# A hybrid encoder layer on one core: which half of a unit runs first, and when the fourth sums of the merged tiles are split

## The chip, the cores and the metric

The kernel runs on one core of a Trainium2 chip. What counts is device time in microseconds (us), from one launch to its end; lower is better. The engines in this text: PE (TensorE, matmuls), DVE (VectorE), ACT (ScalarE), POOL (GpSimd) and SP (SyncE, which issues most DMAs).

## What is computed

One layer over 512 tokens of width 2048, in float32:

```python
hn = rmsnorm(x, norm_g)
proj = jnp.einsum('bsd,dc->bsc', hn, w_in)       # 2048 -> 12 x 512 columns, 4 logits, 3 x 2048 gates
ya = forgetting_attention(qa, ka, va, f_logit)   # three branches of 4 heads of 128
yb = chunked_relpos_attention(qb, kb, vb, rel_bias)
yc = stick_breaking_attention(qc, kc, vc)
ys = jnp.stack([from_heads(ya), from_heads(yb), from_heads(yc)], axis=2)
ys = ys * jax.nn.silu(br[:, :, :, 3])
up = jnp.einsum('bsnw,nwd->bsnd', ys, w_up)      # per branch 512 -> 2048
merged = jnp.sum(gates * up, axis=2)
return x + jnp.einsum('bsd,de->bse', merged, w_out)
```

Nearly all of the work is in three projections: w_in, w_up and w_out.

## The kernel before

**Precision.** A float32 operand is used as a high and a low part (hi and lo; weights: tiles wh and wl). ACT makes the high part by a copy that rounds, DVE subtracts it from the source and so makes the low one (`split`, L243 to L251). A product is hi x hi + hi x lo + lo x hi.

**Units.** PE's work on weights is a list of units. A unit is one 128-column block of weights over eight blocks of 128 rows. For each of the eight, one wide matmul takes wh against the 256 high and 256 low columns of the moving operand (512 columns, into both halves of a PSUM bank), and one narrow matmul takes wl against the 256 high ones (256 columns, into the left half). All eight wide ones run first, then the eight narrow ones. DVE later folds the two halves of the bank together.

**Tasks of seven.** w_in and w_out are multiplied by a Strassen-like scheme (`PairTask`): for two column blocks, two halves of the rows and two halves of the tokens it makes seven products, 1 to 7, instead of eight, so a task is seven units. Products 1, 2, 5, 6, 7, 3, 4 take sums of weights (made by POOL's accumulating DMAs and by DVE in `sums`) against sums of the moving operand. Its usual order is 1, 2, 6, 5, 7, 3, 4. Products 6, 7, 4 and 3 are summed onto the bank that product 1, 6, 7 and 5 left open (`onto`); 1, 2 and 5 open a bank of their own. Two tasks, the first gate task and the first output task, are "late": each product has a bank of its own, and its wh runs as 16 narrow matmuls; the last task ends with one such product (`single`).

**Moving operands.** For w_in these are x1, x2, t23 and t4; for w_out they are m1, m2, m23 and m4 of the merged gates x up (a tile for each of eight pairs of blocks k). The first three of a pair are `Parts` tiles with both token halves; the fourth sum has one half, so two k shared one `Parts` tile. There are 28 tiles for `Parts`; they come free as the tiles of ys are done with (`up_half` for six of them, `up_done` for six more).

**Stages.** First head (in quarters), then heads and gates over w_in (to about 1036 us), then w_up: 16 blocks d in the order k, k + 8 of 36 wide matmuls each, with the gates read back from DRAM (sg) and multiplied in; then eight output tasks from about 1164 us to the end. `merged_a(k)` runs behind block k and `merged_b(k)` behind block k + 8. `merged_b` makes m2, the two third sums (in mt) and the fourth (in mu), waits for `up_half` or `up_done`, splits the third sums into m23 and, after `up_done`, the fourth ones into m4 (`late_t4`).

**The order.** A planner inside the kernel (`Flow`) writes the program: every piece of work is a generator that names its engine, a cost and what it waits for, and the planner keeps a clock for each engine and picks what starts first, by due time. A smaller slack means an earlier due time. PE, DVE and ACT then run exactly in the order written; only semaphores decide when. `stream` walks the units and spawns the preparation (`prep`: wh, then wl) two units ahead.

Of the kernel before, what the change touches and what calls it, by code (L numbers as in the profile page):

```python
# [9 lines left out]
F32R = mybir.dt.float32r  # L10
# [6 lines left out]
S = 512  # L17
# [8 lines left out]
UK = 8  # L26
NQ = 4
HS = S // 2
# [7 lines left out]
PE, ACT, DVE = 0, 1, 2  # L36
# [26 lines left out]
class Flow:  # L63
# [85 lines left out]
def mm_us(n, x=1):  # L149
    return x * max(0.115, n / 2400 + 0.0133)  # L150
# [11 lines left out]
def hybrid_kernel(  # L162
# [31 lines left out]
    flow = Flow()  # L194
    spawn, set_, give = flow.spawn, flow.set, flow.give
# [3 lines left out]
    def t2(s, dt=F32):  # L199
        return tp.tile([P, S], dt, tag="t2", name=nm(s))  # L200
# [19 lines left out]
    def two(ap):  # L220

        return ap.rearrange("p (h s) -> p h s", h=2)
# [19 lines left out]
    def split(hi, lo, src, n, ev=None, due=(), hi_ev=None):  # L242

        yield (ACT, act_us(n), *due)
        nc.scalar.activation(hi, src, AF.Copy)  # L245
        if hi_ev is not None:
            set_(hi_ev)
        yield (DVE, dve_us(n), *due)
        nc.vector.tensor_sub(lo, src, f(hi))  # L249
# [13 lines left out]
    def mm(ps, w, x, start=False, stop=False, more=False):  # L263
        nc.tensor.matmul(ps, w, x, start=start, stop=stop, skip_group_check=more)  # L264
# [87 lines left out]
    class Unit:  # L352


        def __init__(self, mms, after=None, shape=(UK, P), srcs=()):
            self.shape, self.mms, self.after, self.srcs = list(shape), mms, after, srcs
            self.ready_hi, self.ready, self.there, self.raw = Event(), Event(), Event(), None

        def source_there(self):
            return self.there  # L360
# [208 lines left out]
    class Pair(Unit):  # L569


        def __init__(self, task, i):
            super().__init__(task.mms_of(i), task.after_of(i))
            self.task, self.p = task, task.order[i]

        def source_there(self):
            if self is self.task.units[0]:
                spawn(self.task.sums(), 3.0)
            return self.task.there[self.p]

        def source(self):
# [6 lines left out]
    class PairTask:  # L588
# [57 lines left out]
        def mms_of(self, i):  # L646
            p = self.order[i]
            bank = (0, 1, 2, 0, 0, 1, 2)[i] if self.late else {2: 1, 5: 2, 3: 2}.get(p, 0)
            onto = None if self.late else {6: 1, 7: 6, 4: 7, 3: 5}.get(p)
            more = onto is not None  # L650
            single = self.late or self.plain_end and p == 4
            self.bank = getattr(self, "bank", {})
            self.bank[p] = bank

            def go(u):
                if more:
                    yield self.ev[onto]
                    self.ps[p] = self.ps[onto]
                else:
                    yield accs[bank], 1  # L660
                    self.ps[p] = acc(bank)

                for j in range(UK):
                    yield lambda: self.ops[p](j) is not None
                    r, _, ev = self.ops[p](j)
                    yield ev
                    if single:
                        yield PE, mm_us(HS)
                        mm(self.ps[p][:, LH], u.hi[:, j, :], r[:, 0, :], j == 0 and not more, more=more)
                    else:  # L670
                        yield PE, mm_us(S)
                        mm(two(self.ps[p]), u.hi[:, j, :], r, j == 0 and not more, more=more)
                    if single:
                        yield PE, mm_us(HS)
                        mm(self.ps[p][:, LH], u.hi[:, j, :], r[:, 1, :], more=more)
                yield u.ready
                for j in range(UK):
                    yield PE, mm_us(HS)
                    mm(self.ps[p][:, LH], u.lo[:, j, :], self.ops[p](j)[1], stop=j == UK - 1, more=more)
            return go  # L680

        def after_of(self, i):
# [701 lines left out]

        return [Unit(mms(i), shape=(6, P), srcs=[w_up[d, i]]) for i in range(2)]

    m1, m2, m23, m4 = [None] * UK, [None] * UK, [None] * UK, [None] * (UK // 2)
    m4_ev = [Event() for _ in range(UK // 2)]
    kept_m, m1_ev, mus, up_half, up_done = {}, [Event() for _ in range(UK)], {}, Event(), Event()

    def merged_a(k, a):

# [39 lines left out]
    def late_t4(k, u, due):  # L1432
        if k % 2 == 0:
            yield xps, 1
            m4[k // 2] = Parts("m4")
            set_(m4_ev[k // 2])
        yield m4_ev[k // 2]
        h, lo, ev = m4[k // 2].half(k % 2)
        yield from split(h, lo, u, HS, ev, (due + 14.0,))
        if k % 2:  # L1440
            give(t2s)

    for k in range(UK):
        for d in (k, k + UK):
# [4 lines left out]
    at(len(units), freed(xps, 6, up_done))  # L1449


    mops = strassen_ops(m1, m2, m23, m4)

    def out_pair(e):
        evs = [Event(), Event()]
# [71 lines left out]
            yield from load_unit(u)  # L1527

    def stream():
        for i, u in enumerate(units):  # L1530
            cur[0] = i
            for g in side.pop(i, ()):
                spawn(g(), 5.0, flow.fin)
            for j in range(LA + 1) if i == 0 else (i + LA,):
                if j < len(units):
                    spawn(prep(units[j]), 2.5, flow.fin)
            yield u.ready_hi
            yield from u.mms(u)
            if u.after is not None:
                spawn(u.after(), 0.0, flow.fin)  # L1540
# [79 lines left out]
```

## Time and profile before

| | |
|---|---|
| median of 3 runs | 1327.93 us (1326.29 to 1328.51) |
| the profiled execution | 1328.65 us, of it 1326.9 from the first to the last instruction (the span) |
| matmuls | 7506 |
| busy: weight loads, DVE, ACT, POOL | 87%, 86%, 61%, 7% of the span |
| granted TensorE clock | 1.0 all along |
| DMA | 266.24 MB, 201 GB/s on average |

A busy time is the sum of an engine's instruction times. PE's matmuls overlap in its pipeline, so that the busy share says little by itself; the start times of consecutive matmuls say how long one holds up the next. In the views, a row of the timeline is a start in us, a busy time in us, the engine, the line, the tiles (out<-in), and how many instructions the row merges; in brackets stands how long the engine was idle before, and what ended the idle time.

### The profile page before, as it was taken

To read this page: it belongs to the slowest core of one execution; us is meant where nothing else is said; L and a number is where in the kernel's file an instruction comes from. 1 tells how busy PE (TensorE), PEld (TensorE's weight loads), DVE (VectorE), ACT (ScalarE), POOL (GpSimd) and SP (SyncE) were. 2 spreads that over 40 slices of the span, in tenths; PEclk is the share of its full clock that TensorE was granted. 3 is DMA by queue.
4 is the path that set the end of the run, shared out by engine and by line. 5 is a ranking of instruction groups with operands and counts; after the bars stand their busy time and mean duration, and the time that the engine had idled before them with its cause. 6 is when DMAs were issued, how large, how long until landed. Compare 5 with 4: busy or idle time off the path is not lost.

```text
span 1326.9 us, 20238 instructions
## 1 busy us (share of the span) xinstructions
PE 1320.2 (99%) x7506; PEld 1150.5 (87%) x7506; DVE 1134.7 (86%) x1676; ACT 805.9 (61%) x1280; POOL 94.9 (7%) x120
## 2 busy tenths in 40 slices
PE   9999999999999999999999999999999999999998
PEld 6898888888888888888888888888888888888887
DVE  8989888788888889888898979888898877897786
ACT  8767657575556665666656665666557655454443
POOL 0000001000010100000000000000000000001000
PEclk9999999999999999999999999999999999999999
DMA  9776776767786776867878777776779755668893
GB/s 336 207 206 168 190 198 176 212 177 190 200 203 172 197 201 181 219 160 207 200 182 215 173 193 201 192 196 181 194 178 272 278 194 184 193 172 243 235 254 94
DMA packets 89651, 266.24 MB, mean 201 GB/s; under 512 B 10560, under 2 KB 12608, under 8 KB 89552
## 3 DMA queue, kind: packets, MB, share of 16 engines
q1 hardware_dynamic: 70400, 203.86, 46.4%
q0 software_dynamic: 15552, 56.63, 25.8%
q10 hardware_dynamic: 3600, 4.46, 0.9%
q8 instruction: 59, 0.97, 0.3%
q14 instruction: 40, 0.33, 0.1%
HBM read 245.21 MB, written 19.70 MB: 200 GB/s over the span
## 4 chain that ended last, share of the span: by engine, by line
PE 98%; DVE 1%; DMA 0%; issue 0%; DVEq 0%
PE acc L264 84%; PE att L264 8%; PE att L1008 1%; PE att L259 1%; PE att L260 1%; PE att L1121 1%; PE att L1122 1%; PE att L261 1%; PE att L1120 1%; PE att L1072 0%; PE att L1222 0%; DMA begin_in<-in_begin 0%; PE att L909 0%; PE att L910 0%; DVE m L249 0%; DVE wl L249 0%
## 5 line engine op out<-in xcount | busy, mean ns | idle before, releaser
L249 DVE TENSOR_TENSOR wl<-raw,wh 128x1024 fp32r<-128x1024 f32 (+2 forms) x418 | 499.8, 1199 | 141.9 <-ACT wh L245 133.6
L245 ACT ACTIVATE wh<-raw 128x1024 fp32r<-128x1024 f32 (+2 forms) x418 | 434.1, 1039 | 145.3 <-PE acc L264 62.3
L264 PE MATMUL acc<-x,wh 128*128 128x512 f32 (+1 forms) x1568 | 399.2, 391 | 0.7 <-DVE gq L333 0.7
L264 PEld LDWEIGHTS acc<-x,wh 128*128 128x128 f32 x1568 | 277.3, 189 | 50.1 <-issue 2.2
L264 PE MATMUL acc<-t,wh 128*128 128x512 f32 (+1 forms) x1128 | 283.7, 390 | 0.0
L264 PEld LDWEIGHTS acc<-t,wh 128*128 128x128 f32 x1128 | 198.1, 189 | 32.9
L264 PEld LDWEIGHTS acc<-x,wl 128*128 128x128 f32 x1504 | 207.0, 190 | 17.2 <-DVE x L441 0.8
L264 PE MATMUL acc<-x,wl 128*128 128x256 f32 (+1 forms) x1504 | 216.8, 285 | 0.0
L264 PEld LDWEIGHTS acc<-t,wl 128*128 128x128 f32 x1104 | 151.6, 190 | 11.4
L264 PE MATMUL acc<-t,wl 128*128 128x256 f32 x1104 | 155.5, 282 | 0.0
L282 POOL DMA_DIRECT2D raw<-in_w_col x92 | 79.5, 864 | 924.1 <-DMA raw<-in_w_col 573.8
L264 PE MATMUL acc<-m,wh 128*128 128x512 f32 (+1 forms) x512 | 113.7, 366 | 1.5 <-DVE m L249 1.5
L264 PEld LDWEIGHTS acc<-m,wh 128*128 128x128 f32 x512 | 85.4, 190 | 14.4 <-DVE m L249 1.9
L815 ACT ACTIVATE c<-acc 128x256 f32<-128x256 f32 x51 | 19.6, 383 | 97.1 <-PE acc L264 94.1
L782 ACT ACTIVATE u<-acc 128x512 f32<-128x512 f32 x51 | 30.3, 594 | 79.4 <-PE acc L264 79.4
L761 ACT ACTIVATE u<-acc 128x512 f32<-128x512 f32 x52 | 31.1, 598 | 71.9 <-PE acc L264 70.8
L637 DVE TENSOR_TENSOR raw<-raw,raw 128x1024 f32<-128x1024 f32 x54 | 65.9, 1220 | 0.5
L631 DVE TENSOR_TENSOR raw<-raw,raw 128x1024 f32<-128x1024 f32 x54 | 65.8, 1219 | 0.4
L264 PE MATMUL att<-y,wh 128*128 128x512 f32 x256 | 65.8, 389 | 0.0
L264 PEld LDWEIGHTS acc<-m,wl 128*128 128x128 f32 x448 | 60.6, 191 | 3.7
L264 PE MATMUL acc<-m,wl 128*128 128x256 f32 x448 | 62.5, 282 | 0.0
L264 PEld LDWEIGHTS att<-y,wh 128*128 128x128 f32 x256 | 48.0, 188 | 10.0
(207 smaller groups left out, 1397.2 us busy)
## 6 DMA issues: line engine op xcount, KB each, us to landing
raw<-in_w_col SPq DMA_DIRECT2D x230, 512.0 KB, 4.5
raw<-in_w_col POOLq DMA_DIRECT2D x92, 512.0 KB, 6.4
raw<-in_w_out SPq DMA_DIRECT2D x40, 512.0 KB, 5.3
gl<-c SPq DMA_DIRECT2D x48, 256.0 KB, 3.5
raw<-in_w_up SPq DMA_DIRECT2D x32, 384.0 KB, 3.6
sg<-gl SPq DMA_DIRECT2D x48, 256.0 KB, 4.8
raw<-in_w_out POOLq DMA_DIRECT2D x16, 512.0 KB, 6.9
xn<-in_xn SPq DMA_DIRECT2D x16, 256.0 KB, 3.1
```

Source lines behind the costliest of these rows:

```text
L245: nc.scalar.activation(hi, src, AF.Copy)
L249: nc.vector.tensor_sub(lo, src, f(hi))
L259: nc.tensor.matmul(ps, lh, rh, start=start, stop=False, skip_group_check=more)
L260: nc.tensor.matmul(ps, lh, rl, start=False, stop=False, skip_group_check=more)
L261: nc.tensor.matmul(ps, ll, rh, start=False, stop=stop, skip_group_check=more)
L264: nc.tensor.matmul(ps, w, x, start=start, stop=stop, skip_group_check=more)
L282: nc.gpsimd.dma_start(to, src, accum_op=ALU.add)
L631: nc.vector.tensor_add(w[1], w[1], w[5])
L637: nc.vector.tensor_add(w[2], w[2], w[1])
L761: nc.scalar.activation(self.u, ps, AF.Copy)
L782: nc.scalar.activation(self.s, ps, AF.Copy)
L815: nc.scalar.activation(c, ps[:, RH], AF.Copy, scale=-1.0)
```

## The change

**Narrow first.** When a unit of a task begins, `stream` decides in which order its halves run: if the unit adds onto an open bank, the unit just before it in the list ended with its narrow matmuls, and the planner has its wl ready at least `AHEAD` = 0.4 us before PE's clock, it runs its narrow matmuls first and ends with the wide ones. So two narrow halves stand together, and then two wide ones. The first matmul that writes a fresh bank and the last one of the unit carry the start and stop flags as before. The sums of weights are spawned with slack 1.5 instead of 3.0.

**Fourth sums.** `merged_b` no longer keeps the fourth sum in mu: it writes it over the block's own tile, takes a general tile (the pool of 20 tiles of 128 x 512, `t2`) for its high and low part, and splits it at once. m4 has eight such tiles, and they stay until the end. m4 no longer takes four of the `Parts` tiles, and six third sums instead of five start at `up_half`.

```diff
         def __init__(self, task, i):
             super().__init__(task.mms_of(i), task.after_of(i))
             self.task, self.p = task, task.order[i]
+            self.single = task.late or task.plain_end and self.p == 4
+            self.onto = None if task.late else {6: 1, 7: 6, 4: 7, 3: 5}.get(self.p)
 
         def source_there(self):
             if self is self.task.units[0]:
-                spawn(self.task.sums(), 3.0)
+                spawn(self.task.sums(), 1.5)
             return self.task.there[self.p]
...
-                for j in range(UK):
-                    yield lambda: self.ops[p](j) is not None
-                    r, _, ev = self.ops[p](j)
-                    yield ev
...
+                def high(first):
+                    for j in range(UK):
+                        yield lambda: self.ops[p](j) is not None
+                        r, _, ev = self.ops[p](j)
+                        yield ev
+                        start, stop = first and j == 0 and not more, not first and j == UK - 1
...
+                            yield PE, mm_us(S)
+                            mm(two(self.ps[p]), u.hi[:, j, :], r, start, stop, more)
+
+                def low(first):
+                    yield u.ready
+                    for j in range(UK):
+                        yield lambda: self.ops[p](j) is not None
+                        _, x, ev = self.ops[p](j)
+                        yield ev
                         yield PE, mm_us(HS)
-                        mm(self.ps[p][:, LH], u.hi[:, j, :], r[:, 0, :], j == 0 and not more, more=more)
...
+                        mm(self.ps[p][:, LH], u.lo[:, j, :], x, first and j == 0 and not more,
+                           not first and j == UK - 1, more)
+
+                steps = (low, high) if u.low_first else (high, low)
+                for first, step in zip((True, False), steps):
+                    yield from step(first)
...
-        if k % 2 == 0:
-            yield t2s, 1
-            mus[k // 2] = t2("mu")
-        u = mus[k // 2][:, RH if k % 2 else LH]
...
-        minus(u, t[:, LH], b[:, LH])
+        minus(b[:, RH], t[:, LH], b[:, LH])
+        yield t2s, 1
+        parts, ev = t2("m4", F32R), Event()
+        yield from split(parts[:, LH], parts[:, RH], b[:, RH], HS, ev)
         give(t2s)
-        ready = up_half if k < 5 else up_done
+        m4[k] = two(parts), parts[:, LH], ev
+        ready = up_half if k < 6 else up_done
...
-        yield up_done
-        yield from late_t4(k, u, due)
...
             yield u.ready_hi
+            if isinstance(u, Pair) and not u.single:
+                low_there = u.ready.t is not None and u.ready.t + AHEAD <= flow.clock[PE]
+                u.low_first = ends_low and u.onto is not None and low_there
+                ends_low = not u.low_first
+            else:
+                ends_low = False
             yield from u.mms(u)
...
+AHEAD = 0.4
```

What this does to the written order is shown at two places. The first is PE in the second output task (`out_pair(2)`), from the last two narrow matmuls of product 5 to product 7, which adds onto the bank of product 6 (wl_12248 belongs to product 5, wh_12276 and wl_12277 to product 7). Before:

```order
L264 MATMUL acc_12304<-m_2125_11757,wl_12248 128x256
L264 MATMUL acc_12304<-m_2150_11897,wl_12248 128x256
L264 MATMUL acc_12221<-m_2153_11907,wh_12276 128x512
L264 MATMUL acc_12221<-m_2154_11908,wh_12276 128x512
L264 MATMUL acc_12221<-m_2155_11909,wh_12276 128x512
L264 MATMUL acc_12221<-m_2156_11910,wh_12276 128x512
L264 MATMUL acc_12221<-m_2157_11911,wh_12276 128x512
L264 MATMUL acc_12221<-m_2163_11946,wh_12276 128x512
L264 MATMUL acc_12221<-m_2164_11947,wh_12276 128x512
L264 MATMUL acc_12221<-m_2174_12010,wh_12276 128x512
L264 MATMUL acc_12221<-m_2153_11907,wl_12277 128x256
L264 MATMUL acc_12221<-m_2154_11908,wl_12277 128x256
```

Now:

```order
L264 MATMUL acc_12304<-m_2128_11772,wl_12248 128x256
L264 MATMUL acc_12304<-m_2161_11932,wl_12248 128x256
L264 MATMUL acc_12221<-m_2155_11920,wl_12277 128x256
L264 MATMUL acc_12221<-m_2156_11921,wl_12277 128x256
L264 MATMUL acc_12221<-m_2157_11922,wl_12277 128x256
L264 MATMUL acc_12221<-m_2158_11923,wl_12277 128x256
L264 MATMUL acc_12221<-m_2159_11924,wl_12277 128x256
L264 MATMUL acc_12221<-m_2160_11925,wl_12277 128x256
L264 MATMUL acc_12221<-m_2167_11961,wl_12277 128x256
L264 MATMUL acc_12221<-m_2186_12083,wl_12277 128x256
L264 MATMUL acc_12221<-m_2155_11920,wh_12276 128x512
L264 MATMUL acc_12221<-m_2156_11921,wh_12276 128x512
```

The narrow half of product 7 now stands right behind the narrow half of product 5, and its wide half runs on into the wide half of product 3. The second place is DVE in the first output task, around the rows that take products 2 and 3 out of PSUM (c<-u,acc and c<-c,acc; m<-mt is the low part of a third sum, m<-mu that of a fourth). Before:

```order
L717 TENSOR_TENSOR c_2181_12063<-u_11987,acc_12027 128x256
L249 TENSOR_TENSOR wl_12026<-raw_11720,wh_12025 128x1024
L249 TENSOR_TENSOR m_2157_11911<-mt_11535,m_2157_11911 128x2x256
L249 TENSOR_TENSOR m_2163_11946<-mt_11677,m_2163_11946 128x2x256
L249 TENSOR_TENSOR m_2164_11947<-mt_11818,m_2164_11947 128x2x256
L722 TENSOR_TENSOR c_2181_12063<-c_2175_12024,acc_12066 128x256
L249 TENSOR_TENSOR m_2174_12010<-mt_11963,m_2174_12010 128x2x256
L249 TENSOR_TENSOR wl_12065<-raw_11787,wh_12064 128x1024
L249 TENSOR_TENSOR wl_12104<-raw_11824,wh_12103 128x1024
L726 TENSOR_TENSOR u_11987<-u_11987,acc_12105 128x256
L740 TENSOR_TENSOR c_2181_12063<-c_2181_12063,u_11987 128x256
L249 TENSOR_TENSOR m_2165_11949<-mu_10970,m_2165_11949 128x256 x2
```

Now:

```order
L249 TENSOR_TENSOR m_2180_12059<-sg_11809,m_2180_12059 128x256
L730 TENSOR_TENSOR c_2182_12075<-u_11999,acc_12038 128x256
L249 TENSOR_TENSOR wl_12001<-raw_11766,wh_12000 128x1024
L249 TENSOR_TENSOR m_2158_11923<-mt_11401,m_2158_11923 128x2x256
L249 TENSOR_TENSOR m_2159_11924<-mt_11545,m_2159_11924 128x2x256
L249 TENSOR_TENSOR m_2160_11925<-mt_11689,m_2160_11925 128x2x256
L249 TENSOR_TENSOR m_2167_11961<-mt_11829,m_2167_11961 128x2x256
L735 TENSOR_TENSOR c_2182_12075<-c_2176_12035,acc_12078 128x256
L249 TENSOR_TENSOR m_2186_12083<-mt_12019,m_2186_12083 128x2x256
L249 TENSOR_TENSOR wl_12077<-raw_11796,wh_12076 128x1024
L249 TENSOR_TENSOR wl_12115<-raw_11834,wh_12114 128x1024
L739 TENSOR_TENSOR u_11999<-u_11999,acc_12116 128x256
```

The last fourth sum (from sg_11809) is now split before the third sums of blocks 3 to 7, and the other seven stand far above. The wl between the two c is product 6's before and product 3's now; behind it stand four third sums instead of three, and no fourth ones follow.

More of the change, by code (lines that the diff above doesn't have):

```diff
@@ L655, in go @@
             def go(u):
+                single, onto = u.single, u.onto
+                more = onto is not None
                 if more:
@@ L676, in go @@
[L676 to L679, printed above, removed]
+                def high(first):
[4 more added lines that the diff above has]
+                        start, stop = first and j == 0 and not more, not first and j == UK - 1
+                        if single:
+                            yield PE, mm_us(HS)
+                            mm(self.ps[p][:, LH], u.hi[:, j, :], r[:, 0, :], start, stop, more)
+                            yield PE, mm_us(HS)
+                            mm(self.ps[p][:, LH], u.hi[:, j, :], r[:, 1, :], more=more)
+                        else:
+                            yield PE, mm_us(S)
+                            mm(two(self.ps[p]), u.hi[:, j, :], r, start, stop, more)
@@ L1385, in up_units @@
         return [Unit(mms(i), shape=(6, P), srcs=[w_up[d, i]]) for i in range(2)]
-    m1, m2, m23, m4 = [None] * UK, [None] * UK, [None] * UK, [None] * (UK // 2)
-    m4_ev = [Event() for _ in range(UK // 2)]
-    kept_m, m1_ev, mus, up_half, up_done = {}, [Event() for _ in range(UK)], {}, Event(), Event()
+    m1, m2, m23, m4 = [None] * UK, [None] * UK, [None] * UK, [None] * UK
+    kept_m, m1_ev, up_half, up_done = {}, [Event() for _ in range(UK)], Event(), Event()
     def merged_a(k, a):
@@ L1428, in merged_b @@
         give(t2s)
-        yield up_done
-        yield from late_t4(k, u, due)
[L1432 to L1441, printed above, removed]
     for k in range(UK):
@@ L1449, in hybrid_kernel @@
     at(len(units), freed(xps, 6, up_done))
-    mops = strassen_ops(m1, m2, m23, m4)
+    mops = strassen_ops(m1, m2, m23, None)
+    mops[4] = lambda k: m4[k]
     def out_pair(e):
```

13 lines of the change are left out of this document (3 added, 10 removed).

## The prediction

> **What bounds the kernel now.** I read the page first: busy time, then the chain that ended last.
>
> ```profile
> span 1326.9 us, 20238 instructions
> PE 1320.2 (99%) x7506; PEld 1150.5 (87%) x7506; DVE 1134.7 (86%) x1676; ACT 805.9 (61%) x1280; POOL 94.9 (7%) x120
> PE 98%; DVE 1%; DMA 0%; issue 0%; DVEq 0%
> ```
>
> The reader is to see that PE runs without a break and that the chain is PE itself: the time is the sum of the intervals from one matmul's start to the next one's. So the question is what sets an interval, and where PE waits. The second view is PE's timeline (start, busy time, group); I use its start times, because the busy times of pipelined matmuls overlap.
>
> ```profile
> 1186.36 2.00 PE L264 MATMUL acc<-m,wh 128*128 128x512 f32 x8
> 1188.20 1.12 PE L264 MATMUL acc<-m,wl 128*128 128x256 f32 x8
> 1189.15 2.00 PE L264 MATMUL acc<-m,wh 128*128 128x512 f32 x8
> ...
> 1231.05 2.00 PE L264 MATMUL acc<-m,wh 128*128 128x512 f32 x8
> ```
>
> One ordinary unit is eight wide matmuls (512 columns) and eight narrow ones (256). The wide eight take 1188.20 - 1186.36 = 1.84 us, the narrow eight 1189.15 - 1188.20 = 0.95. From 1186.36 to 1231.05 there are 16 units: 44.69 / 16 = 2.793 us each. Now the two widths where they do not alternate, wide in the chain of waits over the w_up stage, narrow in the timeline of the first gate task, whose units run 24 narrow matmuls each:
>
> ```profile
> 1036.18 5.44 PE att L264 x24
> 1041.62 2.72 PE acc L264 x12
> 1044.34 5.44 PE att L264 x24
> ...
> 56.99 2.08 PE L264 MATMUL acc<-x,wh 128*128 128x256 f32 x16
> 58.90 1.12 PE L264 MATMUL acc<-x,wl 128*128 128x256 f32 x8
> ...
> 71.38 0.76 PE L264 MATMUL acc<-t,wh 128*128 128x256 f32 x5
> ```
>
> 36 wide matmuls from 1036.18 to 1044.34 are 226.7 ns each; five units of 24 narrow ones from 56.99 to 71.38 are 14.39 / 120 = 119.9 ns each. Eight of each would be 1.813 + 0.959 = 2.773 us, against 2.793. So a return from narrow to wide costs about 28 ns (1.84 against 1.813), the step from wide to narrow gives about 8 ns back (0.95 against 0.959), and one round of alternation costs 20 ns. That is the price this change goes after. It is no price of a unit's start: the 36 wide matmuls cross unit borders, and so do the 120 narrow ones.
>
> Where PE waits for another engine, from the waits of PE and from the timeline of PE and DVE at the first output task:
>
> ```profile
> PE acc L264 <- DVE m L249: 1.5, 2, 1.3
> ...
> 1175.37 2.08 PE L264 MATMUL acc<-m,wh 128*128 128x256 f32 x16
> 1178.25 2.08 PE L264 MATMUL acc<-m,wh 128*128 128x256 f32 x16
> 1181.13 1.08 PE L264 MATMUL acc<-m,wh 128*128 128x256 f32 x7
> 1182.38 0.84 PE L264 MATMUL acc<-m,wh 128*128 128x256 f32 x4 [0.16 <-DVE m L249]
> 1184.52 1.05 PE L264 MATMUL acc<-m,wh 128*128 128x256 f32 x5 [1.30 <-DVE m L249]
> ...
> 1181.91 0.75 DVE L249 TENSOR_TENSOR m<-mu,m 128x256 fp32r<-128x256 f32 x2
> 1182.91 1.22 DVE L249 TENSOR_TENSOR wl<-raw,wh 128x1024 fp32r<-128x1024 f32 x1
> 1184.05 1.09 DVE L249 TENSOR_TENSOR m<-mu,m 128x256 fp32r<-128x256 f32 x3
> ...
> 1163.00:1187.00 24.00, 22.53 (x176) 21.73 (x175) 23.67 (x40) 12.74 (x22) 0.86 (x1) 1.00 0.63 169
> ```
>
> The last row is a stretch of the windows view: length, then busy PE, weight loads, DVE, ACT, POOL. DVE is busy 23.67 of 24 us, so here DVE is the bound. Product 4 starts at 1181.13 and the next unit at 1186.36: 5.23 us, where 24 narrow matmuls need 2.88. PE loses 2.35 us to the eight late splits of the fourth sums (m from mu).
>
> **Part 1, narrow first.** By the order of the changed program, 134 of the 419 units begin with wl, and the returns from narrow to wide fall from 360 to 230 (wide to narrow from 365 to 228). No matmul is added or taken away. 134 rounds x 20 ns = 2.7 us. Some wide runs are cut by attention matmuls after 3 to 5, so not every ramp was paid whole; with 25 ns a return (130 x 25 = 3.3) less 137 x 8 = 1.1 it is 2.1. Attention groups also stand inside narrow runs now more often than inside wide ones: returns from such a group to wide matmuls fall from 78 to 64, worth 0 to 14 x 28 ns = 0.4. I take **2.4 us**, between 2.0 and 2.8.
>
> What it could cost: the narrow half needs wl, which comes out of ACT's wh and then DVE's subtraction, and it needs it 1.84 us sooner than before. PE runs strictly in order here, so behind a wait for wl stand the unit's wide matmuls and everything after. How early wl is ready, in three places (DVE's subtraction, then the first matmul of its unit):
>
> ```profile
> 1193.74 1.22 DVE L249 TENSOR_TENSOR wl<-raw,wh 128x1024 fp32r<-128x1024 f32 x1
> 1197.53 2.00 PE L264 MATMUL acc<-m,wh 128*128 128x512 f32 x8
> ...
> 127.49 1.21 DVE L249 TENSOR_TENSOR wl<-raw,wh 128x1024 fp32r<-128x1024 f32 x1
> 130.12 1.09 PE L264 MATMUL acc<-t,wh 128*128 128x512 f32 x4
> ...
> 1267.60 1.22 DVE L249 TENSOR_TENSOR wl<-raw,wh 128x1024 fp32r<-128x1024 f32 x1
> ...
> 1028.95 1.22 DVE L249 TENSOR_TENSOR wl<-raw,wh 128x1024 fp32r<-128x1024 f32 x1
> 1030.48 1.78 PE L264 MATMUL acc<-t,wh 128*128 128x512 f32 x7
> ```
>
> 1193.74 + 1.22 = 1194.96, 2.57 us before 1197.53: that is the common case. Set beside the order unit by unit, 14 of the 134 had less than 1.5 us, the first the one at 130.12 (1.42), the last the one at 1270.16 (1.34, from the subtraction at 1267.60), the tightest the one at 1030.48 (0.31). None is below zero, so at DVE's old pace the waits cost 0; if each slipped by one such subtraction (1.13 us from start to start), those with less than that would cost 2.2 us together. I take 0: the sums that are put ahead on DVE (slack 1.5) are no new work, and what they delay there they leave free later.
>
> [...]
>
> **Part 2, the fourth sums.** Each of the eight splits (ACT, then DVE at 1.09 / 3 = 0.36 us) moves from the output task to the place where its sum is made, in the w_up stage; only m4 of the last block stays near the output. DVE has room there: once per block it waits for PE.
>
> ```profile
> 1147.74 0.69 DVE L1368 TENSOR_TENSOR sg<-att,sg 128x512 f32<-128x512 f32 x1 [1.30 <-PE att L264]
> ```
>
> 0.36 into 1.30 us of idle time, every second block: nothing on the path. If that cover were gone, seven splits would be 2.5 us later work on DVE, as before. In return 2.5 us leave the stage in which DVE had 0.33 us to spare, and the 2.35 us wait of product 4 goes. What is late next is the last third sum (m23 of block 7), because six of these instead of five now start at up_half and DVE's queue is written anew. Its needs: product 6 starts at 1175.37 and reads block 7 after 14 narrow matmuls, at 1177.05.
>
> ```profile
> 1172.69 0.42 DVE L717 TENSOR_TENSOR c<-u,acc 128x256 f32<-128x256 f32 x1 [0.23 <-PE acc L264]
> 1173.03 1.22 DVE L249 TENSOR_TENSOR wl<-raw,wh 128x1024 fp32r<-128x1024 f32 x1
> 1174.16 1.89 DVE L249 TENSOR_TENSOR m<-mt,m 128x512 fp32r<-128x512 f32 x3
> 1175.97 0.42 DVE L722 TENSOR_TENSOR c<-c,acc 128x256 f32<-128x256 f32 x1
> 1176.30 0.68 DVE L249 TENSOR_TENSOR m<-mt,m 128x512 fp32r<-128x512 f32 x1
> ```
>
> Before, three third sums (0.60 us apart) and c stood between the wl at 1173.03 and the last third sum, done at 1176.98: 0.07 us to spare. By the new order four stand there. L717 waits for PE's product 2, so it keeps its time. The wl behind it is now product 3's: done at 1173.03 + 1.22 = 1174.25, and needed after 16 narrow matmuls from 1175.37 - 2.88 = 1172.49 on, at 1174.41, so it just fits. Then 1174.16 + 4 x 0.60 + 0.33 = 1176.89, done at 1177.57, and PE resumes about 0.1 us later. That is 0.6 us of new wait. ACT now makes product 6's wh ahead of product 3's, which could push DVE 0.15 us more. I take 0.7: part 2 gives 2.35 - 0.7 = **1.65 us**, between 0.9 (twice that wait) and 2.35 (none).
>
> On SP's queue two gate loads of the last block now stand behind three w_out loads; those were issued by 1141.89 + 8.49 = 1150.4 in the trace before, and the gates are used on DVE from 1162 on, so 11 us hide a landing of 4.8:
>
> ```profile
> 1141.89 8.49 SPq L276 DMA_DIRECT2D raw<-in_w_out  x3
> ...
> 1162.17 0.68 DVE L1368 TENSOR_TENSOR sg<-att,sg 128x512 f32<-128x512 f32 x1
> ...
> sg<-gl SPq DMA_DIRECT2D x48, 256.0 KB, 4.8
> ```
>
> The sum: 2.4 + 1.65 = 4.05, so the profiled execution's span goes to about 1322.9. That execution took 1328.65 us in all; the median of three runs is 1327.93 (1326.29 to 1328.51), 0.7 lower, and I take the gain from the median: 1327.93 - 4.05 = **1323.9 us**.
>
> **The rivals.** (a) The ramp stays: the 28 ns are paid wherever wh follows wl, however long the runs are, or each unit pays it for its new weights. For it: every ramp in the trace but a few stands at a unit's start. Against it: the long runs above show none. Part 1 then gives 0: 1327.93 - 1.65 = 1326.3. (b) DVE is still the bound of the first output task and the wait only changes its place, from product 4 to product 6, at full size. For it: 23.67 of 24 us, and 0.07 us to spare at 1177. Against it: 2.5 us of DVE work leave. Part 2 gives 0: 1327.93 - 2.4 = 1325.5. (c) Slower: PE waits for wl at the tight units. The sums (1.22 us) now have half the slack, and with a 0.69 us add one may stand ahead of wl; a slip of 1.74 us (starts 1.13 and 0.61 apart) on the 14 tight units, whose mean lead is 1.06, costs 14 x 0.68 = 9.5 us, which makes 1327.93 - 4.05 + 9.5 = 1333.4. It decides from a slip of 1.06 + 4.05 / 14 = 1.35 us. Against it: the planner puts narrow first only where it has wl ready 0.4 us ahead, and DVE is idle an eighth of the time in the projections:
>
> ```profile
> 400.00:703.00 303.00, 303.00 (x1758) 266.97 (x1757) 262.21 (x391) 189.81 (x301) 24.20 (x28) 1.00 0.74 191
> ```
>
> **How the numbers follow.** About 0.2% (2.7 us) is what a measurement of this kernel tells from no change, so faster means under 1325.3. The forecast, parts between their bounds (2.9 to 5.2, so 1322.7 to 1325.0), gets 0.64; (a) 0.11; (b) 0.13; (c) 0.09; 0.03 is for what I do not see. Of (b), 0.04 has part 1 at its upper bound and still lands under 1325.3. Faster 0.64 + 0.04 = 0.68; within 0.2% 0.11 + 0.09 + 0.01 = 0.21; slower 0.09 + 0.02 = 0.11. The range runs from the forecast's lower end less the spread of the runs (0.7), 1322.0, over (b) and (a) to 1327.4; what is left out is (c) and a little on either side.
>
> **What would show it.** Step 1: in the ordinary output units two merged units take 5.55 us instead of 5.59, and sixteen wide matmuls run in 3.65 us; if they take 3.68, (a) holds. PE's list of waits should name no wl. Step 2: no wait of PE for m at product 4, and one of about 0.7 us at product 6; DVE in the same stage clearly under 23.67 busy. If the span falls by less than 2.5 us, one of the two parts failed; if it grows, look for PE waiting for DVE's wl at units that begin narrow.

## The result, and the profile after

| | before | after |
|---|---|---|
| median of 7 runs | 1327.92 us (1326.29 to 1328.51) | 1322.29 us (1322.16 to 1324.6) |
| the profiled execution | 1328.65 us, span 1326.9 | 1322.29 us, span 1320.6 |

The ratio after to before is 0.9967, 95% interval 0.9955 to 0.9978: the change makes the kernel faster by 0.2 to 0.45%. The forecast was 1323.9 us; the median came out 1.6 us lower, near the lower end of the range (1322.0).

The page of the changed kernel, in the same lines as before: span, busy times, shares of the chain that ended last.

```profile
span 1320.6 us, 20295 instructions
PE 1314.7 (100%) x7506; PEld 1149.4 (87%) x7506; DVE 1133.8 (86%) x1676; ACT 809.9 (61%) x1280; POOL 95.0 (7%) x120
PE 99%; DMA 1%; DVE 0%; ACT 0%; issue 0%; ACTq 0%
```

The same 7506 matmuls, and the chain is still PE itself. So all of the gain must be in the intervals between matmuls and in PE's waits. First the intervals, in PE's timeline (start, busy time, group) in an output task:

```profile
1186.93 3.82 PE L264 MATMUL acc<-m,wh 128*128 128x512 f32 x16
1190.59 2.08 PE L264 MATMUL acc<-m,wl 128*128 128x256 f32 x16
1192.50 3.82 PE L264 MATMUL acc<-m,wh 128*128 128x512 f32 x16
1196.15 2.08 PE L264 MATMUL acc<-m,wl 128*128 128x256 f32 x16
```

Two units now stand as 16 wide and 16 narrow matmuls. The 16 wide take 1190.59 - 1186.93 = 3.66 us, the 16 narrow 1192.50 - 1190.59 = 1.91; together 5.57 us, where two units took 2 x 2.793 = 5.586 before. Next PE's waits (engine, tile and line, what it waited for; us in total, times, longest) and the first output task:

```profile
PE acc L264 <- DVE gq L333: 1.0, 1, 1.0
PE acc L264 <- DVE m L249: 0.3, 1, 0.3
```

```profile
1168.17 2.08 PE L264 MATMUL acc<-m,wh 128*128 128x256 f32 x16
1170.11 1.22 PE L264 MATMUL acc<-m,wl 128*128 128x256 f32 x8
1171.17 1.96 PE L264 MATMUL acc<-m,wh 128*128 128x256 f32 x15
1173.45 0.39 PE L264 MATMUL acc<-m,wh 128*128 128x256 f32 x1 [0.32 <-DVE m L249]
1173.67 1.12 PE L264 MATMUL acc<-m,wl 128*128 128x256 f32 x8
1174.63 2.08 PE L264 MATMUL acc<-m,wh 128*128 128x256 f32 x16
1177.51 2.08 PE L264 MATMUL acc<-m,wh 128*128 128x256 f32 x16
1180.39 2.00 PE L264 MATMUL acc<-m,wh 128*128 128x512 f32 x8
```

Product 4, which lost 2.35 us before, is the last unit of this task: 1177.51 to 1180.39 is 2.88 us, exactly 24 narrow matmuls. The wait has moved to product 6, which takes 1174.63 - 1171.17 = 3.46 us, 0.58 too many; product 3 ahead of it takes 3.00, 0.12 too many.

### A difference that the change did not make

The two profiled executions differ by 6.33 us in span, more than the forecast had. A third of it stands in the first ten microseconds. PE's timeline at the start, before:

```profile
1.13 3.60 PE L1544 MATMUL att<-tmpc 128*128 128x256 bf16 x16 [1.13 <-POOL tmpc L307]
5.42 1.19 PE L264 MATMUL acc<-x,wh 128*128 128x512 f32 x2 [0.69 <-DVE gq L333]
6.41 1.05 PE L264 MATMUL att<-x,wh 128*128 128x512 f32 x2
...
9.82 0.68 PE L264 MATMUL att<-x,wl 128*128 128x512 f32 x2
10.34 0.62 PE L264 MATMUL acc<-x,wh 128*128 128x512 f32 x2
```

And after:

```profile
1.13 3.22 PE L1551 MATMUL att<-tmpc 128*128 128x256 bf16 x16 [1.13 <-POOL tmpc L307]
5.36 0.70 PE L264 MATMUL acc<-x,wh 128*128 128x512 f32 x2 [1.00 <-DVE gq L333]
5.89 0.63 PE L264 MATMUL att<-x,wh 128*128 128x512 f32 x2
...
8.21 0.63 PE L264 MATMUL acc<-x,wh 128*128 128x512 f32 x2
```

The same matmuls in the same order. Before, a pair of wide ones takes about 0.85 us until 9.82 and 0.46 soon after; after, it takes 0.46 from the second pair on. TensorE's clock had come up at 9.93 us in the one execution and at 3.83 in the other (the clock records of the trace), and the first six pairs show it: 4.92 us from the first real matmul to the seventh pair against 2.85. The windows view gives a PEclk of 1.00 for both, and so does the clock of 1.0 "all along" in the table of the kernel before; the start has to be read from the intervals.

The span by stages, each from the first matmul of one unit to the first of another, in us:

| | before | after | change |
|---|---|---|---|
| launch to the third unit | 13.09 | 10.94 | -2.15 (clock at the start) |
| next seven units | 43.89 | 43.89 | 0 |
| the rest of w_in | 976.28 | 974.15 | -2.13 (narrow first) |
| w_up | 130.59 | 130.56 | -0.03 |
| first output task | 22.50 | 20.85 | -1.65 (fourth sums) |
| seven output tasks, up to the last unit | 134.08 | 133.72 | -0.36 (narrow first) |

So the change itself is worth 4.17 us: 2.13 + 0.03 + 0.36 = 2.52 without the first output task, and 1.65 in it. The runs show the two starts as well: before lies at 1326.29, 1326.49 and at 1327.6 to 1328.51, after at 1322.16 to 1322.29 and at 1324.37 to 1324.6. Low against low is about 4.2 us, high against high 3 to 4. The medians differ by 5.63 since five of seven runs before were high and only three of seven after. The w_up stage, whose idle time was to hide the seven early splits, grew by nothing.

### The profile page after: what moved, and what is told of

It is laid out like the page before. It is cut to its first block, busy times and chain, and to the rows that moved or that the text cites. A ratio compares the mean times of both kernels' runs of the same rounds, so it can differ in the third digit from the quotient of the medians.

```text
span 1320.6 us, 20295 instructions
## 1 busy us (share of the span) xinstructions
PE 1314.7 (100%) x7506; PEld 1149.4 (87%) x7506; DVE 1133.8 (86%) x1676; ACT 809.9 (61%) x1280; POOL 95.0 (7%) x120
## 4 chain that ended last, share of the span: by engine, by line
PE 99%; DMA 1%; DVE 0%; ACT 0%; issue 0%; ACTq 0%
PE acc L264 85%; PE att L264 8%; PE att L1021 1%; PE att L259 1%; PE att L260 1%; PE att L1134 1%; PE att L261 1%; PE att L1135 1%; PE att L1133 1%; PE att L1085 0%; PE att L1235 0%; PE att L922 0%; DMA begin_in<-in_begin 0%; PE att L923 0%; DMA raw<-in_w_out 0%; DVE m L249 0%
## 5 line engine op out<-in xcount | busy, mean ns | idle before, releaser
L264 PEld LDWEIGHTS acc<-x,wh 128*128 128x128 f32 x1568 | 283.2, 188 | 56.2 <-issue 2.2
L264 PE MATMUL acc<-t,wh 128*128 128x512 f32 (+1 forms) x1128 | 280.0, 388 | 0.0
L264 PEld LDWEIGHTS acc<-t,wl 128*128 128x128 f32 x1104 | 144.8, 191 | 1.9
L264 PE MATMUL acc<-m,wh 128*128 128x512 f32 (+1 forms) x512 | 109.7, 364 | 0.3 <-DVE m L249 0.3
L264 PE MATMUL acc<-m,wl 128*128 128x256 f32 x448 | 59.8, 283 | 0.0
```

## The experiments

Eleven runs of ten kernels follow (the last repeats an earlier one). They are compared by the stages of the table above, because single executions differ by up to 2.4 us by their start alone (10.94 to 13.37 us up to the third unit); "w_in" is its row "the rest of w_in" and "rest" its last row.

### Each part alone

Narrow first without the early fourth sums (slack 1.5 kept, the merged tiles' code as before):

```diff
-        parts, ev = t2("m4", F32R), Event()
-        yield from split(parts[:, LH], parts[:, RH], b[:, RH], HS, ev)
+        minus(u, t[:, LH], b[:, LH])
...
-        ready = up_half if k < 6 else up_done
+        ready = up_half if k < 5 else up_done
...
+        yield up_done
+        yield from late_t4(k, u, due)
```

> Part 1 alone: units begin narrow as in the change (136 of 419), the fourth sums are split late, from mu, as before. If the two parts are independent and the price is one of alternation: 1148.6 us from the third unit's start to the first output task (before 1150.77, change 1148.60), the first output task 22.5 us with the 2.35 us wait at product 4 (before 22.50, change 20.85), and the rest of the output tasks as in the change (133.7). If a unit's start pays the ramp whatever the width (rival a), the first stretch stays at 1150.8.

Measured 1325.52 us, the kernel before beside it 1328.88. w_in 974.14, first output task 22.27, rest 133.68: the rows of narrow first are those of the full change (974.15, 133.72), and the first output task is nearly that of before (22.50).

The fourth sums without narrow first (and with slack 3.0):

```diff
-                spawn(self.task.sums(), 1.5)
+                spawn(self.task.sums(), 3.0)
...
-                u.low_first = ends_low and u.onto is not None and low_there
+                u.low_first = False
```

> Part 2 alone: no unit begins narrow, sums with slack 3.0, fourth sums split early into general tiles. Independent parts: 1150.8 us from the third unit to the first output task, 20.85 us in the first output task with a wait of 0.6 us at product 6, 134.1 in the rest. If DVE stays the bound there (rival b), the first output task keeps 22.5 us and product 6 waits 2 us.

Measured 1328.64 us. w_in 976.28 (as before), first output task 20.85 (as after), but rest 135.45: 1.37 us longer than before. The two parts do not touch each other's stage, and something in this kernel takes most of the second part's gain back. PE's timeline in the last output task shows where:

```profile
1305.10 2.00 PE L264 MATMUL acc<-m,wh 128*128 128x512 f32 x8
1306.94 1.11 PE L264 MATMUL acc<-m,wl 128*128 128x256 f32 x8
1308.50 2.10 PE L264 MATMUL acc<-m,wh 128*128 128x512 f32 x8 [0.44 <-ACT wh L245]
1311.01 1.22 PE L264 MATMUL acc<-m,wl 128*128 128x256 f32 x8 [0.40 <-DVE wl L249]
1312.06 2.00 PE L264 MATMUL acc<-m,wh 128*128 128x512 f32 x8
```

PE waits for a high part and then for its low part. Two waits, together 0.84 us, cost 1.37. Idle time counts only from the modelled end of the last matmul, 0.16 us after the point at which the next one could have started (a narrow one is 0.28 busy and holds the next one up for 0.12), and the matmuls after a wait start slower: the eight narrow ones from 1311.01 take 1.05 us, not 0.95, and the eight wide ones from 1308.50 are busy for 2.10, not 2.00. Added to the listed 0.84 us that makes 1.36.

### The slack of the sums

That kernel still had the sums of weights at slack 3.0. So the slack was changed by itself, twice: narrow first off with slack 1.5, and the whole change with slack 3.0.

```diff
-                u.low_first = ends_low and u.onto is not None and low_there
+                u.low_first = False
```

> Part 2 alone, but the sums of weights with slack 1.5 as in the change. If the 1.4 us that part 2 alone lost in the last output task came from the late sums (slack 3.0), the rest of the output tasks is back at 134.1 us; if it came from the eight general tiles that m4 now holds to the end, it stays at 135.4.

```diff
-                spawn(self.task.sums(), 1.5)
+                spawn(self.task.sums(), 3.0)
```

> The whole change with the sums at slack 3.0. If the slack is what the change needs in the last output task, the rest of the output tasks is some 1.4 us longer than the change's 133.72; the first stretch (1148.60) and the first output task (20.85) stay.

Measured 1325.08 and 1325.91 us, before beside them 1328.42. With slack 1.5 and no narrow first the rest is 134.08, as before, and neither wait is there; m4 holds its eight tiles to the end in this kernel too, so they are not what costs the 1.4 us. With slack 3.0 and narrow first it is 135.12, and both waits are back:

```profile
PE acc L264 <- ACT wh L245: 0.5, 1, 0.5
PE acc L264 <- DVE wl L249: 0.4, 1, 0.4
```

DVE and ACT in the last task, slack 3.0 first (the kernel with the fourth sums alone):

```profile
1303.98 1.22 DVE L634 TENSOR_TENSOR raw<-raw,raw 128x1024 f32<-128x1024 f32 x1
1305.46 1.22 DVE L640 TENSOR_TENSOR raw<-raw,raw 128x1024 f32<-128x1024 f32 x1
```

```profile
1305.96 0.60 ACT L774 ACTIVATE u<-acc 128x512 f32<-128x512 f32 x1 [2.50 <-DVE c L1484]
1306.45 2.94 ACT L245 ACTIVATE wh<-raw 128x1024 fp32r<-128x1024 f32 x3
```

And with slack 1.5, whose clock came up early, so that PE runs 2.17 us sooner here (its unit of 1305.10 above, then DVE's first sum):

```profile
1302.93 2.00 PE L264 MATMUL acc<-m,wh 128*128 128x512 f32 x8
```

```profile
1300.35 1.22 DVE L634 TENSOR_TENSOR raw<-raw,raw 128x1024 f32<-128x1024 f32 x1
```

```profile
1301.66 1.06 ACT L245 ACTIVATE wh<-raw 128x1024 fp32r<-128x1024 f32 x1 [0.37 <-DVE raw L634]
...
1304.28 2.00 ACT L245 ACTIVATE wh<-raw 128x1024 fp32r<-128x1024 f32 x2
```

With slack 3.0 the first sum comes 1303.98 - 2.17 - 1300.35 = 1.46 us later against PE, its wh is put behind ACT's copy of acc, and three wh run in a row from 1306.45, of which PE at 1308.50 has waited for the second. With slack 1.5 one of the three is done before that copy. Once the fourth sums are early, then, the small slack is worth 1.4 us. The kernel before had slack 3.0 without this loss: its own order was a different one, so the loss belongs to the new order and not to the slack alone; what in the new order brings it was not tried.

### What a round of alternation costs

If a fixed price stood on every step from narrow to wide, alternating every matmul would show it 2568 times instead of 230. The units that have wl ready run wide and narrow in turn; the other parts stay:

```diff
+                def both():
...
+                        mm(two(self.ps[p]), u.hi[:, j, :], r, j == 0 and not more, more=more)
+                        yield PE, mm_us(HS)
+                        mm(self.ps[p][:, LH], u.lo[:, j, :], x, stop=j == UK - 1, more=more)
...
-                u.low_first = ends_low and u.onto is not None and low_there
+                u.low_first, u.alternate = False, low_there
```

> The change with wide and narrow matmuls in turn (one of each, eight times) in every ordinary unit where wl is ready, 349 of them, none narrow first. If each step from narrow to wide has a fixed price (28 ns, less 8 back), the eight rounds of a unit cost 160 ns instead of 20: a unit takes 2.93 us and the kernel about 49 us more than before, 1377 us. If the price is a ramp over the first five wide matmuls after a narrow run (233, 236, 228, 232, 231 ns) and the return lies in the first two narrow ones (113, 119), a round of one each costs 233 + 113 = 346 ns, a unit 2.77 us, and the kernel about 4 us less than the change, 1318 us.

Measured 1329.46 us; w_in 977.36 and rest 135.50, 1.1 and 1.4 us over before: neither the large loss of a price per step nor the gain of the other estimate. PE's timeline, 18 rounds, then 16 rounds of other units:

```profile
599.63 0.40 PE L264 MATMUL acc<-t,wh 128*128 128x512 f32 x1
599.87 0.28 PE L264 MATMUL acc<-t,wl 128*128 128x256 f32 x1
599.98 0.40 PE L264 MATMUL acc<-t,wh 128*128 128x512 f32 x1
...
605.99 0.40 PE L264 MATMUL acc<-t,wh 128*128 128x512 f32 x1
...
621.00 0.39 PE L264 MATMUL acc<-t,wh 128*128 128x512 f32 x1
...
626.55 0.39 PE L264 MATMUL acc<-t,wh 128*128 128x512 f32 x1
```

(605.99 - 599.63) / 18 = 353 ns for one wide and one narrow, against 2.793 / 8 = 349 in groups of eight before and 226.7 + 119.9 = 347 in long runs. The second stretch has (626.55 - 621.00) / 16 = 347 ns, no more than long runs. Both kinds are common: of the 246 unbroken stretches of eight rounds in this trace, 100 take 2.77 to 2.79 us (347 ns a round) and 146 take 2.81 to 2.91 (354 on average); over all of them a round costs 351 ns. So strict alternation costs 0 or 7 ns a round over long runs, 4 on average, and not 20. In the changed kernel the 16 wide matmuls after narrow ones take 233, 236, 228, 232 and 231 ns, then 227 each. So in grouped runs the loss is spread over the first five or so wide matmuls: a group of eight pays it once, 20 ns a unit after what its narrow ones win back, and a group of 16 half as often. That the wide matmuls lose more than the narrow ones win back is measured; why, and why alternating stretches come in two kinds, is not.

### The condition on wl

The condition `low_there` was taken away, so that narrow comes first wherever the list of units allows it:

```diff
-                u.low_first = ends_low and u.onto is not None and low_there
+                u.low_first = ends_low and u.onto is not None
```

> The change without the condition that wl be ready 0.4 us ahead: 155 units begin narrow instead of 134. Alternation alone: 21 rounds x 20 ns = 0.4 us less than the change. If wl at these units is late on the chip (rival c), PE's waits name wl and the time rises by up to 21 x 0.3 = 6 us.

Measured 1330.52 us, w_in 980.19, 6.04 more than after. 155 units begin narrow instead of 134, and PE's waits name wl:

```profile
PE acc L264 <- DVE wl L249: 4.7, 7, 0.7
```

Seven waits of 0.67 us in the list; from start to start each takes 0.955 us where 0.120 is usual, so they cost 5.8 us. This is the wait that rival (c) feared, and in the change the 0.4 us of `AHEAD` keep it out. The other way round, a stricter condition:

```diff
-AHEAD = 0.4
+AHEAD = 2.0
```

> The change with AHEAD = 2.0 us: 99 units begin narrow instead of 134, the returns from narrow to wide are 266 (before 360, change 230). If part 1 is a price per return, its gain is 94 / 130 of the change's 2.53 us, 1.8 us: stretch and rest together 0.7 us longer than in the change. If the tight units' waits had eaten a share of the gain, dropping them would cost less than that, or nothing.

Measured 1325.26 us. 99 units begin narrow and 266 returns (steps from narrow to wide) are left of 360; w_in 974.60 and rest 133.85, so 1.68 + 0.23 = 1.91 us less than before, for 94 returns fewer: 20.3 ns each. The full change has 130 fewer and 2.52 us: 19.4 each. Narrow first alone: 132 fewer, 2.14 + 0.40 = 2.54, 19.2 each. Against the kernel with slack 1.5 and no narrow first, which differs from the change in nothing else and has 364 returns in its trace, the change has 134 fewer and gains 2.04 + 0.36 = 2.40 us (976.19 to 974.15, 134.08 to 133.72): 17.9 each. Over these counts the gain goes with the number of returns, at 18 to 20 ns.

### The wait that is left at product 6

In the first output task, DVE reaches the last third sum late because block 7's fourth sum is split ahead of it, though product 4 comes after product 6. It was put behind:

```diff
+        def fourth(*due):
+            yield t2s, 1
...
+        if k < UK - 1:
+            yield from fourth()
         ready = up_half if k < 6 else up_done
...
         give(t2s)
+        if k == UK - 1:
+            yield from fourth()
```

> The change with the fourth sum of the last pair of blocks split behind its third sums, not ahead of them. If DVE's queue sets the 0.6 us wait that is left at product 6, the wait falls to 0.2 to 0.3 us and the first output task to about 20.5 us; all else as in the change.

Measured 1321.88 us; the first output task takes 20.41 us, and m is no longer among PE's waits. Of the 0.44 us that are won, product 3 gives its 0.12 and product 6 the rest; product 6 still takes 3.14 us, 0.26 over 24 narrow matmuls. The time is the lowest single one of the study, with a clock that came up early, at 4.15 us.

### The clock at the start

In all executions profiled so far the clock was full either at 3.8 to 4.9 us or at 9.2 to 10.4. Between the last of the 16 warm-up matmuls (which ends at 4.4 to 4.7 us) and the first real one PE stands idle for 0.7 to 1.2 us, waiting for gq. Three kernels were timed side by side: the change with 20 warm-ups, the same with block 7's fourth sum last, and the latter with 16.

```diff
-WARM = 16
+WARM = 20
```

> The changed kernel with 20 warm-up matmuls at the start instead of 16; nothing else is different. In the executions profiled so far TensorE reaches its full clock either at 3.8 to 4.9 us, while the warm-up matmuls still run, or at 9.2 to 10.4 us, and the second kind is 2.2 us longer whatever the kernel. Between the last warm-up matmul (about 4.7 us) and the first real one (5.4 to 5.9 us) TensorE stands idle for 0.7 to 1.2 us. Theory G (the gap breaks the run of work that the clock waits for): four more warm-ups at 0.22 us fill the gap until about 5.6 us; the clock is full by 7 us at the latest, no run lies near 1324.5, all lie between 1322.0 and 1323.3. Rival H (the clock comes up by a phase that the gap has no part in): both kinds remain, about half of the runs near 1322.2 and the rest near 1324.5. Rival I (the added warm-ups delay the first real matmul): all runs later by 0.2 to 0.9 us.

> The changed kernel with the fourth sum of block 7 split last, as in m4_7_last, and 20 warm-up matmuls. Theory: the two are independent. The first output task takes 20.4 us instead of 20.85, so the runs lie 0.4 us under those of warm20: by theory G all between 1321.6 and 1322.9, median about 1321.9; by rival H about half near 1321.8 and half near 1324.0; by rival I everything 0.2 to 0.9 us later.

> m4_7_last once more, with 16 warm-up matmuls, timed often beside the two runs with 20. Theory G: two kinds of runs remain, near 1321.8 and near 1324.0, 2.2 us apart, and its median is the one or the other by chance; the lowest run is level with the lowest of last_and_warm. Against the kernel before at the same start it is 4.5 us shorter (4.1 for the whole change and 0.4 for block 7).

| | runs, us | median | full clock at |
|---|---|---|---|
| change, 20 warm-ups | 1322.5, 1322.77, 1322.97, 1323.13, 1323.3 | 1322.97 | 6.25 |
| block 7 last, 20 warm-ups | 1321.92, 1322.15, 1322.21, 1322.46 | 1322.18 | 5.32 |
| block 7 last, 16 warm-ups | 1322.14, 1322.5, 1323.78, 1324.21, 1324.43 | 1323.78 | 8.95 |
| before, 16 warm-ups | 1326.32, 1326.87, 1327.07 and six from 1327.89 to 1329.13 | 1328.04 | |

A fifth run of the second row took 3150.76 us, for a reason that is not known, and is left out. PE's timeline with 20 warm-ups:

```profile
1.13 4.45 PE L1551 MATMUL att<-tmpc 128*128 128x256 bf16 x20 [1.13 <-POOL tmpc L307]
5.49 1.05 PE L264 MATMUL acc<-x,wh 128*128 128x512 f32 x2
6.38 0.62 PE L264 MATMUL att<-x,wh 128*128 128x512 f32 x2
```

No idle time is left ahead of the first real matmul (0.22 us in the other kernel with 20), and only the first pair runs slow. With the gap filled, none of the nine runs lies in the late kind, while the kernels with 16 warm-ups show both kinds side by side on the same chip. So filling the gap is what ends the late starts, as theory G forecast. Of a delay by the added warm-ups (rival I) the first real matmul shows nothing: it starts at 5.49 and 5.74 us, where it started at 5.36 to 5.95 with 16. But the best early starts are not reached either. The change with 20 warm-ups lies at 1322.50 to 1323.30, above its early runs with 16 at another time (1322.16 to 1322.29): in the profiled execution the slow first pair and the start cost 0.42 us up to the third unit (11.36 for 10.94), and w_in takes 974.40 for 974.15.

The gap alone does not decide it: with 16 warm-ups PE has it in early executions as well (1.00 us idle where the clock came up at 3.83 us, 0.69 us where it came up at 9.93), so something differs from launch to launch, and to that extent rival H is right too. In the traces of before and after the record of the full clock is 1317.55 us long both times, though the spans are 1326.9 and 1320.6 us. What sets the moment of the rise, and how much idle time ahead of it matters, was not shown. Theory G's reason, a run of work that the clock waits for, was not shown either; shown is that with no gap or 0.22 us of it the clock was full at 6.25 and 5.32 us, and that none of the nine runs was late.

The best kernel of the study is the change with block 7's fourth sum last and 20 warm-ups: ratio to before 0.9954 (0.9941 to 0.9968), against 0.9967 (0.9955 to 0.9978) for the change alone. The intervals overlap; what is shown is that its first output task is 0.44 us shorter and that its late starts are gone.

## Why the prediction was right, and where it was not

**Narrow first: right in mechanism and size.** Forecast 2.4 us, measured 2.52 against the kernel before and 2.40 (w_in and rest) against the one of equal slack. The kernels with 94, 130 and 132 returns fewer than before give 19 to 20 ns each, the comparison at equal slack 18; the prediction had 20. Rival (a), the ramp stays, is out: the sixteen wide ones take 3.66 us, not 3.68, and from the sixth on each takes 227 ns, through the border of the two units. The mark of 5.55 us for two units was added up wrong: joining two units saves one round of the two, 5.586 - 0.020 = 5.566, and 5.57 was measured. What a wide matmul takes goes with what stood before it: after narrow ones 233, 236, 228, 232 and 231 ns, and then 227. But 20 ns is the price of a group of eight, not of a step; taken as the price of a step it fails by far in the alternating kernel.

**No wait for wl: right.** PE's waits name none. The kernel without the condition shows what it guards against: 6 us in w_in. Rival (c) needed a slip of 1.35 us. In the change nothing of it reached PE: at all 111 places where 16 narrow matmuls of two units stand together, the second unit's first one starts 120 ns after the one before it.

**The fourth sums: right in path and size, to the hundredth by luck.** Forecast 1.65 us, measured 1.65. The wait at product 4 is gone, and the new one is at product 6, at its sixteenth matmul. The forecast had 0.7 us of it there; 0.58 are there, and 0.12 at product 3's narrow half, for which the forecast had wl "just fit". DVE's rows show why:

```profile
1166.91 1.23 DVE L249 TENSOR_TENSOR wl<-raw,wh 128x1024 fp32r<-128x1024 f32 x1 [0.19 <-ACT wh L245]
1168.16 0.42 DVE L249 TENSOR_TENSOR m<-sg,m 128x256 fp32r<-128x256 f32 x1
1168.51 0.41 DVE L730 TENSOR_TENSOR c<-u,acc 128x256 f32<-128x256 f32 x1
1168.84 1.22 DVE L249 TENSOR_TENSOR wl<-raw,wh 128x1024 fp32r<-128x1024 f32 x1
1169.97 2.49 DVE L249 TENSOR_TENSOR m<-mt,m 128x512 fp32r<-128x512 f32 x4
1172.38 0.41 DVE L735 TENSOR_TENSOR c<-c,acc 128x256 f32<-128x256 f32 x1
1172.71 0.68 DVE L249 TENSOR_TENSOR m<-mt,m 128x512 fp32r<-128x512 f32 x1
```

Behind product 3's wl (1168.84) come four third sums, c, and the last third sum, done at 1173.39; PE goes on at 1173.45. This is the row of the forecast, moved by the 4.31 us that the stage begins earlier (1163.85 to 1159.54), and 0.13 late. The forecast let c of L717 (now L730) start by PE's product 2, which would be 1172.69 - 4.31 = 1168.38; but DVE had waited 0.19 us for ACT's wh of product 6 (the push of 0.15 us that the forecast names), so c comes behind block 7's fourth sum (m<-sg) at 1168.51. On the other side the forecast put the need at product 6's fifteenth matmul, which reads the high part; the low part, which DVE makes, is read by the sixteenth, 0.12 us later. These errors nearly cancel. Rival (b), the wait at full size in another place, is out.

**DVE's busy time: a mark that did not come.** The prediction said that DVE would be busy clearly less than 23.67 of 24 us in that stage. The windows view over exactly the first output task (length, then busy PE, weight loads, DVE), before and after:

```profile
1163.85:1186.36 22.51, 21.04 (x169) 20.48 (x168) 22.18 (x38) 11.89 (x21) 0.86 (x1) 1.00 0.61 164
```

```profile
1159.54:1180.39 20.85, 20.53 (x170) 20.26 (x168) 20.50 (x33) 11.11 (x16) 0.86 (x1) 1.00 0.58 165
```

DVE is busy 22.18 of 22.51 us before (98.5%) and 20.50 of 20.85 after (98.3%). It does fewer pieces (33 for 38), but the stage is shorter by as much, and DVE stays as full as it was. The lateness of one piece was what had to go, not the busy share.

**The slack of the sums: a step costed at 0 that was not 0.** The prediction said that the sums put ahead on DVE are no new work and leave later what they delay. In w_in that is so (976.19 with slack 1.5 and 976.28 before). But in the last output task it saves 1.4 us, against a loss that the early fourth sums would have brought and that the prediction did not see. The two cancel (rest 134.08 both before and with slack 1.5), and so the sum came out right, by luck, with one gain and one loss missing.

**The median: the step that failed.** The prediction took its 4.05 us from the median of before as if all runs started alike, and read the 2.2 us between the lowest and highest run as noise. Its span, about 1322.9, is 0.2 us off once the start is put right: 1320.57 + 2.15 = 1322.72. Of the 1.6 us by which the median missed, 0.1 is the size of the gain (4.17 for 4.05); the rest is the start of the clock: by the two groups of runs the median of before is a late start and that of after an early one. That 1322.29 still lies in the range is owed to the 0.7 us of spread taken off its lower end, 1322.7. Before's timeline showed the late start, in pairs of wide matmuls 0.85 us apart until 9.82, ahead of everything that the prediction quoted.

## What to carry to other kernels

When runs of one kernel differ by about 2 us again and again, look at the first matmuls of the profiled execution before subtracting a gain from a median; and let warm-up matmuls run up to the first real one, with no gap (none of nine such runs started late). A price read from one pattern (20 ns for a round of eight) is a price of that pattern: group, alternate and lengthen the runs before carrying it over. Where work is moved in a queue that is written by due time, compare every later stage too: the piece that comes late may be 140 us further on.

## What the runs showed of the hardware that was not expected

- TensorE's clock came up at 3.8 to 4.9 or at 8.95 to 10.4 us with a gap of 0.7 to 1.2 us in PE's early work, and at 6.25 and 5.32 us with no gap or 0.22 us of it. Late executions reach the third unit at 12.78 to 13.37 us, early ones at 10.94 to 11.30.
- Wide matmuls after narrow ones are slow for about five (233, 236, 228, 232, 231 ns, then 227). One by one in turn with narrow ones, a round costs 347 ns in some stretches, as in long runs, and 354 in others, 351 on average.
- A listed wait of PE cost more than its idle time: 0.32 us listed, 0.58 lost at product 6; 0.84 listed, 1.37 lost in the last task of the kernel with the fourth sums alone.
